# Down projection of a hybrid decoder layer: weight combinations made in place, own raw buffers for every second block, eight output spots held in PSUM

## The chip, the core and the metric

The kernel runs on one core of a Trainium2 chip. Its engines are TensorE (PE, with its weight loads as PEld), VectorE (DVE), ScalarE (ACT), GpSimd (POOL) and SyncE (SP, which here only issues transfers). Each works through a queue of its own in order. The metric is device time in microseconds of one launch, the median of several runs.

## The reference

One layer of a decoder over 1024 tokens and 16 learned ones in front, all in float32: a normalisation, one wide input projection, four token mixers (a gated recurrence, a multi-scale pooling, a stick-breaking attention, a short convolution), a gated merge with an output projection, and then the part that this change touches, with 1024 columns and 4096 hidden columns:

```python
h2 = rmsnorm(x, norm2_g)
act = jnp.square(jax.nn.relu(jnp.einsum('bld,df->blf', h2, w_up)))
return x + jnp.einsum('blf,fd->bld', act, w_down)
```

and a last normalisation of the result.

## The kernel before

Every float32 operand of a matmul is split in two (L74, L75): ACT casts it to a rounded high part, DVE subtracts that from it for the low part, and three matmuls (high with high, high with low, low with high) stand for one. DVE's operation at L75 has two SBUF inputs.

The hidden columns are 32 rows of 128. The down projection sums over them: the first 4 rows in the standard way, the other 28 by Strassen's scheme in Winograd's form, with 7 products for 8.

**Standard rows** (L948 to L963). The output is 16 spots: 8 blocks of 128 tokens by 2 halves of 512 columns, kept in SBUF in x1, which also holds the residual. `down_std` sums two rows for each spot in one PSUM bank (6 matmuls) and DVE adds the bank to x1 (L957). It is called twice, for rows 0 and 1 and for rows 2 and 3 (L1065); the second pass uses the banks "z" and "tr". There are eight banks: "mm" three, "z" two, "tr" two, "av" one. The later rows' operands were loaded early ("early", L880) and are split into the "wa" buffers at L962.

**Strassen rows** (L968 to L1104). 28 rows are 14 blocks of two, each 256 hidden columns; a group c is two blocks, so there are 7 groups. For a block, `down_w` loads two rows of w_down into w1 and w2 (L972, L973, by SP). Their halves are b11, b12 (w1) and b21, b22 (w2). The seven right-hand operands of the products are b11, b21, b22 and four combinations: b12 - b11, b22 minus that, b22 - b12, and b21 minus the second. POOL makes the four (L981, L983, L984, L988), and ACT and DVE split everything into the pair h, l of 7 x 512 columns (`put`). The pairs lie in "wb" for groups 0, 2, 4, 6 and in "wa" for the others, so those of group c + 1 can be written as soon as group c - 1 is done with them. The raw tiles w1 and w2 take the two buffers "raw"; the first two combinations go to a third tile "ta" in a buffer "hi".

A group has four units m, each for two token blocks. A unit's left-hand sums come from DRAM: `down_s` loads one tile (s_raw, one buffer) and splits it into s_hi ("wide" is its low part) and a late part ("lo" or "s_late"). Then 7 products of 6 matmuls follow; their order over two units is 1 and 5 of a unit, 7 of the unit before, 6, 2 and 3 of the unit, 4 of the unit before. DVE adds results to x1 (L1021 to L1039); product 6 accumulates in the bank that L1021 reads after product 1, so it must wait for that add.

The code's order is not the queues' order: a scheduler at build time places the instructions of each engine by priority and a model of its own. Buffers of a tag are handed round, and whoever writes one waits for the last user.

Of the kernel before, what the change touches and what calls it, by code (L numbers as in the profile page):

```python
# [10 lines left out]
F32 = mybir.dt.float32  # L11
# [6 lines left out]
P = 128  # L18
D = 1024
# [5 lines left out]
NB = T // P  # L25
# [19 lines left out]
def hybrid_trunk_kernel(ctx: ExitStack, tc: tile.TileContext, x_tok, metas, vecs, gains, w_in, w_br, w_pool,  # L45
                        w_o, w_up, w_dn, lvl_mask, out):
    nc = tc.nc

    def pool(name, bufs=1, side=None, stack=ctx):
        return stack.enter_context(tc.tile_pool(name=name, bufs=bufs, side=side, reuse_waits="tile"))  # L50

    const = pool("const")
    wst = pool("wst", 2)
# [6 lines left out]
    def nm(s):  # L60
        serial[0] += 1
        return f"{s}_{serial[0]}"

    def bank(tag):
        return psum.tile([P, 512], F32, tag=tag, name=nm(tag), bufs=PSUM_BUFS[tag])

    def new(pl, shape, dt, tag, bufs=None):
        return pl.tile(shape, dt, tag=tag, name=nm(tag), **({} if bufs is None else {"bufs": bufs}))
# [27 lines left out]
    def mm3(ps, lhs, rhs, first, last):  # L96
        lh, ll = lhs
        rh, rl = rhs
        nc.tensor.matmul(ps, lh, rh, start=first, stop=False)  # L99
        nc.tensor.matmul(ps, lh, rl, start=False, stop=False)  # L100
        nc.tensor.matmul(ps, ll, rh, start=False, stop=last)  # L101
# [96 lines left out]
    with ExitStack() as st:  # L198
# [159 lines left out]
        for i, (c0, n) in enumerate(FCH):  # L358
            last = i == len(FCH) - 1
# [25 lines left out]
        for i in range(NS + 2):  # L385
            parts, z, r = [], iter(()), i % (2 * NB)
            if i < NS:
# [9 lines left out]
                z = steps[i].scores(i)  # L397
# [50 lines left out]
    with ExitStack() as st:  # L448
# [35 lines left out]
        for hd in range(HEADS):  # L484
# [36 lines left out]
            for half in range(2):  # L521
                ps = bank("z")
# [3 lines left out]
            for li, h in enumerate(LEVELS):  # L526
# [8 lines left out]
                ps = bank("z")  # L535
# [31 lines left out]
            ps = bank("tr")  # L567
            nc.tensor.matmul(ps[:, :P], kt[:NM, NB, :], v[:NM, NB, :], start=True, stop=True)
            nc.vector.tensor_copy(S[:, NB - 1, :], ps[:, :P])
            for c1 in (NB, NB // 2):  # L570
                ps = bank("tr").rearrange("p (b c) -> p b c", c=P)
# [138 lines left out]
    with ExitStack() as st:  # L710
        p2 = pool("prep", 1, None, st)
        u = None
        for k in range(4):
# [6 lines left out]
            u = pool_diff(p2, k, v)  # L720
# [6 lines left out]
    with ExitStack() as st:  # L727
# [38 lines left out]
        for u, (n, d0) in enumerate(units):  # L766
            outs = [new(p2, [P, T], F32, "go", 3) for _ in range(2)]

            def put(r, c, ps, add):
                dst = outs[r][:, c * 512:(c + 1) * 512]  # L770
                if add is None:
                    nc.scalar.activation(dst, ps, AF.Sigmoid)
                else:
                    nc.vector.tensor_add(dst, ps, add)
                    nc.scalar.activation(dst, dst, AF.Sigmoid)
# [48 lines left out]
    with ExitStack() as st:  # L824
        x1 = new(pool("x1", 1, None, st), [P, NB, D], F32, "x1")
# [3 lines left out]
        for eh in range(2):  # L829
            es = slice(eh * 512, (eh + 1) * 512)  # L830
            wh, wl = wo0 if eh == 0 else load_wo(1, wst, "raw")
            for b in range(NB):
# [3 lines left out]
                ps = bank("mm")  # L836
# [18 lines left out]
    with ExitStack() as st:  # L855
# [41 lines left out]
        for f in range(FS):  # L897
# [4 lines left out]
            for c0, n in QCH:  # L902
                cs = slice(c0, c0 + n)
                ps = bank("mm")
# [8 lines left out]
        for f in range(FS, NF, 2):  # L913
# [17 lines left out]
            if f + 2 == NF:  # L931
                eng = nc.sync
                x1 = new(dn, [P, NB, D], F32, "x1", 1)
# [11 lines left out]
        h2stack.close()  # L945
        dw = pool("down", 4)

        def down_std(rows, tags):  # L948
            n = len(rows)
            for b in range(NB):  # L950
                bs = slice(b * P, (b + 1) * P)
                for eh in range(2):
                    es = slice(eh * 512, (eh + 1) * 512)
                    ps = bank(tags[(2 * b + eh) % len(tags)])
                    for i, (act, wd) in enumerate(rows):
                        mm3(ps, (act[0][:, bs], act[1][:, bs]), (wd[0][:, es], wd[1][:, es]), i == 0, i == n - 1)
                    nc.vector.tensor_add(x1[:, b, es], x1[:, b, es], ps)  # L957

        down_std(rows, ("z", "tr", "mm", "z", "tr", "mm", "mm"))
        act2, wd2 = (pair_of(dw, ("wa", "wa"), 4, [P, 7 * 512]) for _ in range(2))  # L960
        rows = [tuple(tuple(t[:, i * D:(i + 1) * D] for t in ab) for ab in (act2, wd2)) for i in range(2)]
        for i, t in enumerate(early):  # L962
            split(*rows[i // 2][i % 2], t)  # L963

        TI = {1: 0, 2: 1, 3: 2, 5: 3, 6: 4, 7: 5, 4: 6}
        SI = {1: 0, 5: 1, 2: 2, 6: 3, 3: 4, 7: 5, 4: 6}

        def down_w(u):  # L968
            h, l = pair_of(dw, (("wb", "wb"), ("wa", "wa"))[u // 2 % 2], 4, [P, 7 * 512])
            f = FS + 2 * u  # L970
            w1, w2 = new(wst, [P, D], F32, "raw"), new(wst, [P, D], F32, "raw")
            nc.sync.dma_start(w1, w_dn[f])  # L972
            nc.sync.dma_start(w2, w_dn[f + 1])  # L973
            b11, b12, b21, b22 = w1[:, :512], w1[:, 512:], w2[:, :512], w2[:, 512:]
            ta = new(wst, [P, D], F32, "hi")

            def put(c0, src):
                sl = (slice(None), slice(c0, c0 + src.shape[1]))
                split(h[sl], l[sl], src)

            nc.gpsimd.tensor_sub(ta[:, :512], b12, b11)  # L981
            put(0, b11)
            nc.gpsimd.tensor_sub(ta[:, 512:], b22, ta[:, :512])  # L983
            nc.gpsimd.tensor_sub(b12, b22, b12)  # L984
            put(512, w2)
            put(1536, ta)
            put(2560, b12)
            nc.gpsimd.tensor_sub(b21, b21, ta[:, 512:])  # L988
            put(3072, b21)
            return h, l  # L990

        def down_s(c, m):
# [10 lines left out]
        class Unit:  # L1003
# [7 lines left out]
            def prod(self, ps, i, fresh=False):  # L1011
                for k, (th_, tl_) in enumerate(self.tw):
                    rs, ls = slice(TI[i] * 512, (TI[i] + 1) * 512), slice(SI[i] % 5 * P, (SI[i] % 5 + 1) * P)
                    sh, sl = (t[:, k, ls] for t in self.s[SI[i] // 5])
# [47 lines left out]
                final(self.m, 1)  # L1062

        NU = (NF - FS) // 2
        down_std(rows, ("z", "tr"))  # L1065

        fg, outs = None, None

# [12 lines left out]
        prev, last = None, NU // 2 - 1  # L1081
# [83 lines left out]
```

## Time and profile before

| | us |
|---|---|
| median of three runs | 2033.37 (2032.72 to 2042.26) |
| profiled execution, its own time | 2038.52 |
| its span | 2036.8 |
| mean granted clock of TensorE in it | 0.993 |

Down projection in the profile: from 1694.89 us to the end. In the views below, L-numbers are lines of the kernel; a tile's name stands without its number; "out<-in" is what an instruction writes and reads; "[1.00 <-X]" is the idle time of the engine before it, and what ended that. In the list of stretches the columns are the length, then busy time and count for PE, PEld, DVE, ACT and POOL, the granted clock, the share of the DMA engines and GB/s (where one engine was asked for, only that one).

### The profile page before, as it was taken

The numbers are of one execution on the slowest core, as the hardware profiler recorded it, in microseconds if no ns is written. First come the engines' busy times: TensorE is split into PE (matmuls) and PEld (weight loads), VectorE is DVE, ScalarE is ACT, GpSimd is POOL, SyncE is SP. The second block draws the span as 40 slices with busy tenths as digits, with TensorE's granted clock in tenths as the row PEclk, the third lists the DMA queues.
The fourth block names the chain that finished last, engine by engine and source line by source line (L and its number), as shares of the span: only waits on it lengthen the run. The fifth ranks groups of instructions, "written<-read, shape, count | busy, mean of one in ns | idle before, by whom it ended". The sixth has DMA issues, their size and how long they took to land.

```text
span 2036.8 us, 25928 instructions
## 1 busy us (share of the span) xinstructions
PE 1947.2 (96%) x9972; PEld 1657.5 (81%) x9972; DVE 1352.2 (66%) x1797; ACT 866.2 (43%) x1481; POOL 379.1 (19%) x346
## 2 busy tenths in 40 slices
PE   7989989999999899999999999999999999899998
PEld 6778788888889898888887888887788888678876
DVE  6778887668777964333333567479555556888887
ACT  6566665433332323434433122255454553434435
POOL 3121212200010002333330000001332221432322
PEclk9999999999999999999999999999999999999999
DMA  3100000201101222332334655142445556444443
GB/s 136 42 32 22 32 32 22 69 22 42 53 22 41 72 85 77 124 120 88 124 124 174 219 181 186 48 155 82 146 135 160 162 147 232 149 138 139 160 134 131
DMA packets 109916, 216.76 MB, mean 106 GB/s; under 512 B 7888, under 2 KB 58576, under 8 KB 109792
## 3 DMA queue, kind: packets, MB, share of 16 engines
q1 hardware_dynamic: 55696, 171.54, 25.0%
q10 hardware_dynamic: 54096, 43.56, 6.5%
q8 instruction: 78, 1.28, 0.3%
q14 instruction: 46, 0.38, 0.1%
HBM read 153.73 MB, written 61.34 MB: 106 GB/s over the span
## 4 chain that ended last, share of the span: by engine, by line
PE 72%; DVE 13%; issue 6%; ACT 3%; DMA 3%; POOL 2%; SPq 0%; POOLq 0%; DVEq 0%; ACTq 0%
PE mm L672 15%; PE mm L100 10%; PE mm L101 10%; PE mm L99 10%; PE z L672 8%; PE tr L672 4%; PE mm L1016 4%; PE z L1016 2%; DVE keep L312 2%; PE z L545 1%; DMA raw<-in_w_dn_dram 1%; PE av L336 1%; PE tr L1016 1%; DVE wa L75 1%; PE tr L323 1%
## 5 line engine op out<-in xcount | busy, mean ns | idle before, releaser
L99 PE MATMUL mm<-h_hi,hi 128*128 128x384 f32 (+4 forms) x1008 | 351.9, 350 | 0.8 <-ACT a L177 0.6
L101 PE MATMUL mm<-h_hi,lo 128*128 128x384 f32 (+4 forms) x1008 | 346.7, 344 | 4.2 <-DVE lo L75 4.2
L100 PE MATMUL mm<-h_lo,hi 128*128 128x384 f32 (+4 forms) x1008 | 347.3, 345 | 0.7 <-DVE h_lo L75 0.7
L101 PEld LDWEIGHTS mm<-h_hi,lo 128*128 128x128 f32 x1008 | 191.7, 190 | 17.1 <-DVE lo L75 4.9
L100 PEld LDWEIGHTS mm<-h_lo,hi 128*128 128x128 f32 x1008 | 191.9, 190 | 12.5 <-DVE h_lo L75 1.2
L99 PEld LDWEIGHTS mm<-h_hi,hi 128*128 128x128 f32 x1008 | 191.5, 190 | 12.4 <-ACT a L177 0.9
L649 POOL TENSOR_TENSOR sf<-raw 128x512 f32<-128x512 f32 x30 | 41.7, 1390 | 784.7 <-DVE eh L615 341.4
L75 DVE TENSOR_TENSOR sl<-sf,sh 128x1024 fp32r<-128x1024 f32 x60 | 74.4, 1241 | 106.2 <-ACT sh L74 106.2
L75 DVE TENSOR_TENSOR lo<-raw,hi 128x1024 fp32r<-128x1024 f32 x79 | 98.8, 1251 | 53.2 <-ACT hi L74 43.3
L74 ACT CAST hi<-raw 128x1024 fp32r<-128x1024 f32 x79 | 83.1, 1052 | 102.9 <-PE mm L100 68.3
L99 PE MATMUL mm<-b_hi,eh 128*128 128x512 f32 x256 | 100.2, 392 | 1.9 <-DVE mixed L812 1.9
L100 PE MATMUL mm<-b_lo,eh 128*128 128x512 f32 x256 | 100.8, 394 | 0.1
L101 PE MATMUL mm<-b_hi,el 128*128 128x512 f32 x256 | 100.3, 392 | 0.5 <-DVE el L75 0.5
L672 PE MATMUL mm<-th,sh 128*128 128x512 f32 x240 | 94.1, 392 | 5.0 <-ACT cc L677 5.0
L74 ACT CAST sh<-sf 128x1024 fp32r<-128x1024 f32 x60 | 63.0, 1052 | 72.6 <-PE z L672 34.7
L672 PE MATMUL mm<-tl,sh 128*128 128x512 f32 x240 | 93.9, 391 | 0.0
L672 PE MATMUL mm<-th,sl 128*128 128x512 f32 x240 | 93.9, 391 | 0.0
L312 DVE TENSOR_TENSOR_SCAN keep<-keep 128x1039 f32<-128x1039 f32 (+3 forms) x64 | 88.9, 1393 | 6.9 <-ACT keep L305 3.3
L310 POOL TENSOR_SCALAR_AFFINE_SELECT keep<-keep 128x128 f32<-128x128 f32 x64 | 34.5, 539 | 260.2 <-ACT keep L305 225.9
L75 DVE TENSOR_TENSOR at_l<-tr,at_h 128x384 fp32r<-128x384 f32 (+2 forms) x112 | 62.6, 567 | 22.5 <-ACT at_h L74 20.1
L323 PE MATMUL tr<-ident,sig 128*128 128x128 f32 x352 | 56.6, 276 | 21.1 <-DVE sig L313 15.0
L75 DVE TENSOR_TENSOR el<-raw,eh 128x512 fp32r<-128x512 f32 x30 | 31.9, 1064 | 64.5 <-ACT eh L74 61.4
(389 smaller groups left out, 4974.7 us busy)
## 6 DMA issues: line engine op xcount, KB each, us to landing
raw<-in_w_in_dram SPq DMA_DIRECT2D x76, 512.0 KB, 3.8
s_raw<-sum_dram SPq DMA_DIRECT2D x28, 896.0 KB, 4.8
gate_dram<-go ACTq DMA_DIRECT2D x32, 512.0 KB, 2.6
go<-gate_dram SPq DMA_DIRECT2D x32, 512.0 KB, 3.4
raw<-in_w_up_dram SPq DMA_DIRECT2D x32, 512.0 KB, 3.8
raw<-in_w_dn_dram SPq DMA_DIRECT2D x31, 512.0 KB, 4.7
sum_dram<-go ACTq DMA_DIRECT2D x52, 256.0 KB, 4.5
sum_dram<-sums ACTq DMA_DIRECT2D x39, 256.0 KB, 4.6
```

Of the source, the lines that this page charges most:

```text
L74: nc.scalar.copy(hi, src)
L75: (eng or nc.vector).tensor_sub(lo, src, hi.bitcast(F32))
L99: nc.tensor.matmul(ps, lh, rh, start=first, stop=False)
L100: nc.tensor.matmul(ps, lh, rl, start=False, stop=False)
L101: nc.tensor.matmul(ps, ll, rh, start=False, stop=last)
L310: nc.gpsimd.affine_select(out=t, in_=t, compare_op=ALU.is_gt, fill=fill, base=0, pattern=[[1, P]], channel_multiplier=-1)
L312: nc.vector.tensor_tensor_scan(kp[:, 1:n], kp[:, 1:n], kp[:, 1:n], 1.0, op0=ALU.mult, op1=ALU.min)
L323: nc.tensor.transpose(ps[:, b, :], self.sg[:, (b0 + b) * P:(b0 + b + 1) * P], ident)
L336: nc.tensor.matmul(av[:, :w], pair.vv[e][:, b, :], a[:, b, :w], start=i == 0 and a is at[0], stop=i == len(order) - 1 and a is at[1])
L649: nc.gpsimd.tensor_add(s12[:, 0], a21, a22)
L672: nc.tensor.matmul(ps, lhs[i][x][:, k, :], rhs[i][y][:, k, :], start=fresh and k == 0 and n == 0, stop=k == 3 and n == 2, skip_group_check ...
L1016: nc.tensor.matmul(ps, x, y[:, rs], start=fresh and k == 0 and n == 0, stop=k == 1 and n == 2, skip_group_check=not fresh)
```

## The change

Three things. In `down_w` the four combinations are made in place: b12 - b11 overwrites b11 (L987), b22 - b12 overwrites b12 (L988), and so on (L990, L991); "ta" is gone, the splits are four in place of five (512, then three times 1024 columns), and two of the seven operands change places in the pair (the table TI). Each in-place subtraction follows the split of what it overwrites. The raw tiles of every second block (u odd) take the two buffers "hi" in place of "raw". In the standard rows the first pass finishes only spots 0 to 7; spots 8 to 15 stay in the eight banks, without an add, and the second pass adds its rows to them there first; the other eight spots of the second pass use "av", "z" and "tr". Each of the spots 8 to 15 thus has one add in place of two.

```diff
-        down_std(rows, ("z", "tr", "mm", "z", "tr", "mm", "mm"))
+        spots = [(b, slice(eh * 512, (eh + 1) * 512)) for b in range(NB) for eh in range(2)]
+
+        def down_std(rows, spot, ps, first=True, last=True):
+            b, es = spot
+            bs = slice(b * P, (b + 1) * P)
+            for i, (act, wd) in enumerate(rows):
+                mm3(ps, (act[0][:, bs], act[1][:, bs]), (wd[0][:, es], wd[1][:, es]), first and i == 0,
+                    last and i == len(rows) - 1)
+            if last:
+                nc.vector.tensor_add(x1[:, b, es], x1[:, b, es], ps)
+
+        held = []
+        for i, spot in enumerate(spots):
+            ps = bank(("z", "tr", "mm", "z", "tr", "mm", "mm", "av")[i % 8])
+            down_std(rows, spot, ps, last=i < 8)
+            if i >= 8:
+                held.append((spot, ps))
...
-        TI = {1: 0, 2: 1, 3: 2, 5: 3, 6: 4, 7: 5, 4: 6}
+        TI = {1: 0, 2: 1, 3: 2, 5: 3, 7: 4, 4: 5, 6: 6}
...
-            w1, w2 = new(wst, [P, D], F32, "raw"), new(wst, [P, D], F32, "raw")
+            w1, w2 = (new(wst, [P, D], F32, ("raw", "hi")[u % 2]) for _ in range(2))
...
-            ta = new(wst, [P, D], F32, "hi")
...
-            nc.gpsimd.tensor_sub(ta[:, :512], b12, b11)
             put(0, b11)
-            nc.gpsimd.tensor_sub(ta[:, 512:], b22, ta[:, :512])
+            put(512, w2)
+            nc.gpsimd.tensor_sub(b11, b12, b11)
             nc.gpsimd.tensor_sub(b12, b22, b12)
-            put(512, w2)
-            put(1536, ta)
-            put(2560, b12)
-            nc.gpsimd.tensor_sub(b21, b21, ta[:, 512:])
-            put(3072, b21)
+            put(1536, w1)
+            nc.gpsimd.tensor_sub(b22, b22, b11)
+            nc.gpsimd.tensor_sub(b21, b21, b22)
+            put(2560, w2)
...
-        down_std(rows, ("z", "tr"))
+        for spot, ps in held:
+            down_std(rows, spot, ps, first=False)
+        for i, spot in enumerate(spots[:8]):
+            down_std(rows, spot, bank(("av", "z", "tr")[i % 3]))
```

What the scheduler makes of it is shown at three places. The first is DVE in group 2, from the first split of a block for group 3 (wa, from raw) to the next unit's s tile (wide, lo). L1021 is the add after product 1, L1023 after 5, L1027 after 7, L1031 after 6, L1039 after 4. Before:

```order
L75 TENSOR_TENSOR wa_15137<-raw_15138,wa_15136 128x512
L1039 TENSOR_TENSOR x_2122_13999<-mm_14798,x_2122_13999 128x512
L75 TENSOR_TENSOR wa_15137<-raw_15139,wa_15136 128x1024
L1021 TENSOR_TENSOR tr_14964<-mm_14962,x_2122_13999 128x512
L1023 TENSOR_TENSOR x_2122_13999<-z_14963,x_2122_13999 128x512
L75 TENSOR_TENSOR wa_15137<-hi_15142,wa_15136 128x1024
L1027 TENSOR_TENSOR x_2122_13999<-mm_14901,x_2122_13999 128x512
L75 TENSOR_TENSOR wide_15017<-s_raw_15014,s_hi_15016 128x1280
L1031 TENSOR_TENSOR x_2122_13999<-mm_14962,x_2122_13999 128x512
L75 TENSOR_TENSOR lo_15020<-s_raw_15014,lo_15020 128x512
L75 TENSOR_TENSOR wa_15137<-raw_15138,wa_15136 128x512
```

After the change the same place reads (L1024, L1026, L1030, L1034, L1038 and L1042 are the adds after products 1, 5, 7, 6, 3 and 4):

```order
L1024 TENSOR_TENSOR tr_14930<-mm_14928,x_2122_13999 128x512
L75 TENSOR_TENSOR wa_15103<-raw_15104,wa_15102 128x512
L1026 TENSOR_TENSOR x_2122_13999<-z_14929,x_2122_13999 128x512
L75 TENSOR_TENSOR wa_15103<-raw_15105,wa_15102 128x1024
L1030 TENSOR_TENSOR x_2122_13999<-mm_14867,x_2122_13999 128x512
L75 TENSOR_TENSOR wa_15103<-raw_15104,wa_15102 128x1024
L1034 TENSOR_TENSOR x_2122_13999<-mm_14928,x_2122_13999 128x512
L75 TENSOR_TENSOR wa_15103<-raw_15105,wa_15102 128x1024
L1038 TENSOR_TENSOR x_2122_13999<-z_14929,x_2122_13999 128x512
L75 TENSOR_TENSOR wide_14983<-s_raw_14980,s_hi_14982 128x1280
L1042 TENSOR_TENSOR x_2122_13999<-mm_14867,x_2122_13999 128x512
L75 TENSOR_TENSOR lo_14986<-s_raw_14980,lo_14986 128x512
```

The block's four splits now stand together between the adds of one unit, and "wide" of the next unit stands behind the last of them; before, two of the five came after "wide".

The second place is ACT at the same point, with the casts of the high parts. Before:

```order
L74 CAST wa_15136<-raw_15138 128x512
L74 CAST wa_15136<-raw_15139 128x1024
L74 CAST wa_15136<-hi_15142 128x1024
L74 CAST wa_15136<-raw_15138 128x512
L74 CAST s_hi_15016<-s_raw_15014 128x1280
L74 CAST lo_15020<-s_raw_15014 128x512
L74 CAST wa_15136<-raw_15139 128x512
L1033 COPY x_2122_13999<-tr_14964 128x512
```

and after, where wa_15102 is the pair of the first block and wa_15120 that of the second, which is read from the buffers "hi":

```order
L74 CAST wa_15102<-raw_15104 128x512
L74 CAST wa_15102<-raw_15105 128x1024
L74 CAST wa_15120<-hi_15122 128x512
L74 CAST wa_15120<-hi_15123 128x1024
L74 CAST wa_15102<-raw_15104 128x1024
L74 CAST wa_15102<-raw_15105 128x1024
L1036 COPY x_2122_13999<-tr_14930 128x512
L74 CAST s_hi_14982<-s_raw_14980 128x1280
L74 CAST lo_14986<-s_raw_14980 128x512
```

The casts of the second block's untouched halves moved up to the first block's, and s_hi of the next unit moved behind all casts of the first block.

The third place is DVE at the passes of the standard rows. Before, from the last three adds of the first pass (mm_14128, z_14136, tr_14144) on into the second pass, with splits of rows 2 and 3 (wa) and of block 0 (wb):

```order
L957 TENSOR_TENSOR x_2122_13999<-x_2122_13999,mm_14128 128x512
L75 TENSOR_TENSOR wa_14155<-s_raw_13975,wa_14154 128x1024
L957 TENSOR_TENSOR x_2122_13999<-x_2122_13999,z_14136 128x512
L957 TENSOR_TENSOR x_2122_13999<-x_2122_13999,tr_14144 128x512
L75 TENSOR_TENSOR wa_14153<-s_late_13976,wa_14152 128x1024
L75 TENSOR_TENSOR wa_14155<-raw_13977,wa_14154 128x1024
L75 TENSOR_TENSOR wb_14293<-raw_14294,wb_14292 128x512
L957 TENSOR_TENSOR x_2122_13999<-x_2122_13999,z_14164 128x512
L957 TENSOR_TENSOR x_2122_13999<-x_2122_13999,tr_14172 128x512
L957 TENSOR_TENSOR x_2122_13999<-x_2122_13999,z_14180 128x512
```

After, at the last adds of the held spots (mm_14130, av_14137) and the first of the other eight (z_14220, av_14212), with block 0 (from raw) and block 1 (from hi):

```order
L957 TENSOR_TENSOR x_2122_13999<-x_2122_13999,mm_14130 128x512
L75 TENSOR_TENSOR wb_14277<-raw_14279,wb_14276 128x1024
L957 TENSOR_TENSOR x_2122_13999<-x_2122_13999,av_14137 128x512
L75 TENSOR_TENSOR wb_14295<-hi_14296,wb_14294 128x512
L957 TENSOR_TENSOR x_2122_13999<-x_2122_13999,z_14220 128x512
L75 TENSOR_TENSOR wb_14295<-hi_14297,wb_14294 128x1024
L957 TENSOR_TENSOR x_2122_13999<-x_2122_13999,av_14212 128x512
L957 TENSOR_TENSOR x_2122_13999<-x_2122_13999,tr_14228 128x512
L75 TENSOR_TENSOR wb_14295<-hi_14296,wb_14294 128x1024
```

Block 1's splits, which stood near the end of the second pass, now stand in its middle, and the add that frees the bank "av" stands behind the last split of block 0.

More of the change, by code (lines that the diff above doesn't have):

```diff
@@ L946, in hybrid_trunk_kernel @@
         dw = pool("down", 4)
[L948 to L957, printed above, removed]
-        down_std(rows, ("z", "tr", "mm", "z", "tr", "mm", "mm"))
+        spots = [(b, slice(eh * 512, (eh + 1) * 512)) for b in range(NB) for eh in range(2)]
[13 more added lines that the diff above has]
+                held.append((spot, ps))
         act2, wd2 = (pair_of(dw, ("wa", "wa"), 4, [P, 7 * 512]) for _ in range(2))
```

## The prediction

> **What bounds the kernel now.** First the page, for the span and the engines' shares; then the table of stretches, for how much TensorE (PE) loses in which stage; then the waits of PE alone, and the timeline around them.
>
> ```profile
> span 2036.8 us, 25928 instructions
> PE 1947.2 (96%) x9972; PEld 1657.5 (81%) x9972; DVE 1352.2 (66%) x1797; ACT 866.2 (43%) x1481; POOL 379.1 (19%) x346
> 1694.89:1738.75 43.86, 43.86 (x194) 35.97 (x193) 36.01 (x48) 12.72 (x16) 7.39 (x5) 1.00 0.69 244
> 1738.75:1784.24 45.49, 38.36 (x158) 29.92 (x156) 39.77 (x46) 20.21 (x26) 21.25 (x12) 0.96 0.41 140
> 1784.24:1985.42 201.18, 193.82 (x842) 158.35 (x840) 171.81 (x210) 83.92 (x110) 57.53 (x39) 0.99 0.41 142
> 1985.42:2036.80 51.38, 41.57 (x181) 33.44 (x179) 38.63 (x82) 25.80 (x58) 10.68 (x8) 0.96 0.36 132
> PE mm L1016 <- DVE tr L1021: 11.7, 7, 3.6
> PE mm L1016 <- ACT s_hi L74: 2.4, 1, 2.4
> ```
>
> PE sets the time. The four stretches are the two standard passes, group 0, groups 1 to 5, and group 6 with the ending. In the stretches' rows the first time is the length, then PE, PEld, DVE, ACT, POOL busy. The passes have no gap in PE. A group is 4 units of 7 products of 6 matmuls. A product takes 1.36 us, as the chain shows:
>
> ```profile
> 1872.20 2.72 PE mm L1016 x12
> 1874.92 1.36 PE z L1016 x6
> 1881.72 2.72 PE mm L1016 x12
> ```
>
> So a unit is 9.52 us and a group 38.1. Group 0 takes 45.5 and so loses 7.4; groups 1 to 5 take 201.2 against 190.4 and lose 10.8 together, 2.2 each. Most of that is the wait for the add at L1021, which VectorE (DVE) reaches late:
>
> ```profile
> 1744.19 0.50 PE L1016 MATMUL mm<-wb,s_hi 128*128 128x512 f32 x1 [2.44 <-ACT s_hi L74]
> 1744.53 0.40 PE L1016 MATMUL z<-wb,s_hi 128*128 128x512 f32 x1
> 1744.77 0.40 PE L1016 MATMUL z<-wb,wide 128*128 128x512 f32 x1
> 1746.58 0.73 PE L1016 MATMUL mm<-wb,s_hi 128*128 128x512 f32 x2 [0.72 <-DVE tr L1021]
> 1777.25 1.22 PE L1016 MATMUL mm<-wb,s_hi 128*128 128x512 f32 x2 [3.63 <-DVE tr L1021]
> 1978.23 1.15 PE L1016 MATMUL mm<-wa,s_hi 128*128 128x512 f32 x2 [2.16 <-DVE tr L1021]
> 1777.00:1778.00 1.00, 0.75 (x2) 0.50 0.00 0
> 1778.00:1779.00 1.00, 1.00 (x4) 0.50 0.00 0
> ```
>
> Of the 11.7 us in seven waits, 0.72 and 3.63 lie in group 0, which leaves 7.4 for groups 1 to 5. Behind the longest waits the granted clock is 0.50 for about 3.2 us: after 1777.25 the matmuls come every 0.43 us for 0.23, and 1.6 us are lost once more. It happened after 3.63 and after 2.16 us, and not after 2.44, where the matmuls at 1744.53 and 1744.77 are 0.24 apart. 7.4 and one such 1.6 make 9.0; the other 1.8 of the 10.8 is 0.36 a group in small pieces.
>
> **The change, part by part.** Work first. PE's matmuls are the same. DVE loses eight adds of the first pass (0.6 us each, 4.8) and one split in five per block, with the same number of columns. GpSimd (POOL) keeps four subtractions a block. None of that is on the path by itself: no pass had a gap.
>
> *Loads.* The blocks' loads waited on SP for the last use of the two raw buffers:
>
> ```profile
> SPq L972 <- DVE wb L75: 34.5, 7, 11.9
> 1887.32 1.30 POOL L981 TENSOR_TENSOR hi<-raw 128x512 f32<-128x512 f32 x1 [10.11 <-DMA raw<-in_w_dn_dram]
> 1887.81 2.16 DVE L75 TENSOR_TENSOR wide<-s_raw,s_hi 128x1280 fp32r<-128x1280 f32 x1
> 1888.69 2.42 POOL L983 TENSOR_TENSOR hi<-raw,hi 128x512 f32<-128x512 f32 x1
> ```
>
> The second block of a group now has its own two, so its load lies there early. That removes the first cause of the late L1021: the second block's subtractions and splits no longer arrive in a heap with the load. It gains at most the 18 us lost in groups 0 to 5.
>
> The last two rows also price POOL against DVE. The split at 1887.81 takes 1.48 us elsewhere (1878.81, below); here it waits 0.8 for POOL's op to end at 1888.62. POOL's next takes 2.42 for 1.30: it waits until the split is through. I take it that a DVE operation on two SBUF tensors and a POOL operation run one after the other, and that whoever waits is next.
>
> *In place.* This is the dear part. Before, the first block's three subtractions ran as soon as its load was there, long before its slots were free, with DVE half idle; one was left for the busy unit:
>
> ```profile
> 1863.12 1.29 POOL L981 TENSOR_TENSOR hi<-raw 128x512 f32<-128x512 f32 x1 [6.56 <-DMA raw<-in_w_dn_dram]
> 1865.74 1.29 POOL L984 TENSOR_TENSOR raw<-raw,raw 128x512 f32<-128x512 f32 x1
> 1872.69 1.57 ACT L74 CAST wb<-raw 128x512 fp32r<-128x512 f32 x2 [1.22 <-PE mm L1016]
> 1873.35 0.69 DVE L75 TENSOR_TENSOR wb<-raw,wb 128x512 fp32r<-128x512 f32 x1 [0.42 <-ACT wb L74]
> 1874.56 1.21 DVE L75 TENSOR_TENSOR wb<-raw,wb 128x1024 fp32r<-128x1024 f32 x1
> 1875.69 0.69 DVE L1021 TENSOR_TENSOR tr<-mm,x 128x512 f32<-128x512 f32 x1
> 1875.91 1.29 POOL L988 TENSOR_TENSOR raw<-raw,hi 128x512 f32<-128x512 f32 x1 [8.88 <-DVE wb L75]
> 1877.47 1.27 ACT L74 CAST s_hi<-s_raw 128x1280 fp32r<-128x1280 f32 x1 [1.74 <-DMA s_raw<-sum_dram]
> 1878.81 1.48 DVE L75 TENSOR_TENSOR wide<-s_raw,s_hi 128x1280 fp32r<-128x1280 f32 x1
> 1880.40 0.59 ACT L1033 COPY x<-tr 128x512 f32<-128x512 f32 x1 [0.62 <-PE tr L1016]
> ```
>
> Now the first subtraction overwrites b11, so it must wait for DVE's low part of b11, which waits for ACT's high part, which waits for the slot (1872.69). All four subtractions, 5.2 us, move behind that point. And the order of the engines puts the splits of both halves ahead of what the next unit needs: on ACT, the cast of w2 (behind POOL's fourth) stands ahead of s_hi; on DVE, the w2 split ahead of "wide". PE cannot start the next unit without s_hi.
>
> I walk it with the durations above on the clock of the group that begins at 1862.68, in the order of groups 2 to 5. Steps of DVE are 0.6 for an add or 512 columns, 1.13 for 1024, 1.40 for 1280; of ACT 1.05 for 1024, 0.5 for the copy, 1.25 for s_hi. Product 1 of the second unit ends at 1874.92; the third unit is due 6 products later, at 1883.08.
> - DVE: L1024 to 1875.6, b11 low part to 1876.2.
> - POOL 1: to 1877.6. DVE's w2 split waits for it: to 1878.7.
> - POOL 2: to 1880.0; POOL 3: to 1881.3. ACT's w1 cast to 1881.1, DVE's w1 split to 1882.4.
> - POOL 4 waits for that: to 1883.8. ACT's w2 cast to 1884.8, copy to 1885.3, s_hi to 1886.5.
>
> PE is 3.45 us late. Then 5 matmuls (1.1 us) fit in before "wide", which DVE ends at 1888.0 (w2 split to 1886.0, an add): 0.35 more, **3.8** in all. The second block repeats it one unit on: DVE has its b11 low part at 1890.6, POOL ends at 1892.0, 1894.4, 1895.7 and 1898.1, s_hi at 1901.0, and PE is free at 1896.4: **4.6**. In group 1 the order has b11 ahead of L1024, and the same walk gives 3.1 and 4.3.
>
> Sum for groups 1 to 5: 7.4 + 4 x 8.4 = 41.0 of stalls; one slow-clock stretch a group, 5 x 1.6 = 8.0; the small pieces 1.8. That is 50.8 in place of 10.8: **+40**.
>
> A rule against the row: the Trainium skill (TensorE: Matmul & The Clock Gate, "What's actually happening") halves the clock after an idle window of about 3.4 us. By it both stalls of a group would bring a slow stretch, 5 x 1.6 = 8 us more than I sum. This trace had one already after 2.16 us of idle and none after 2.44, so I stay with one a group.
>
> *Held spots and group 0.* Spots 8 to 15 keep all eight banks until the second pass ends them. Before, DVE waited for the late half of x1, and group 0 for its second block:
>
> ```profile
> 1711.77 0.69 DVE L957 TENSOR_TENSOR x<-x,tr 128x512 f32<-128x512 f32 x1 [3.92 <-DMA x<-x_dram]
> 1736.42 1.29 POOL L981 TENSOR_TENSOR hi<-raw 128x512 f32<-128x512 f32 x1 [6.55 <-DMA raw<-in_w_dn_dram]
> ```
>
> The first wait goes, but hid nothing on PE. The second, with the 2.44 that it led to, should go. But the new order puts the add of the last held spot (bank "av") behind the first block's w2 split. PE begins the second pass at 1716.65 (16 spots of 1.36 after 1694.89), ends the held spots at 1727.5, and DVE has the block's b11 low part after the third held add, at 1721.9. From there to the end of the w2 split the walk above took 9.8 us: 1731.7, and the add ends at 1732.3. PE needs the bank at 1729.1 and waits 3.3 us. The second block's chain begins after the add, at 1732.95, and ends at 1742.8; behind it stand three adds, "wide", a low part and L1024, 4.4 us, so that group 0's third product starts at 1747.2 for 1746.58. Inside group 0 the next block has its b11 at 1747.8, and s_hi of unit 2 ends at about 1757.6 where PE wants it at 1752.7 (four products on): 5.0. "Wide" comes behind parts of one block more, at about 1761.2, 2.7 later than PE wants it. So 0.6 and 7.7 come for the 3.63 and 1.6 that go: +3, and a slow stretch of 1.6 is likely. I take **+5**, between 0 (no lock, below) and +8 (more than one slow stretch).
>
> Sum: +45 on the profiled execution's 2038.52 gives 2083.5. Its time lies 5.2 above the median of the three runs, 2033.37, so the forecast against that median is **2078**.
>
> **The rivals.**
> - *The chain without the lock.* If DVE and POOL do not hold each other up, POOL runs 1876.3 to 1881.5, s_hi is 1.2 late and "wide" 0.35; at the second block 2.15. Groups 1 to 5 then lose 5 x 3.7 + 1.8 = 20.3 for 10.8, group 0 nothing: +10, **2043**. Against it stand 1887.81 and 1888.69. The Trainium skill (SBUF — State Buffer, "SBUF: two separate sides") calls this port pair an exclusive lock held for the whole instruction, by which this case cannot come; the two rows agree.
> - *The early load wins: faster.* Mechanism: the second block's load is off SP's wait, and the whole of the 18 us goes. **2015**. It decides where POOL's fourth subtraction ends before about 1880.2, so that ACT's w2 cast, copy and s_hi end by 1883.08. For it: the 34.5 us of waits of L972. Against: four subtractions of 1.29 after 1876.2 end at 1881.4 at best.
> - *Even.* Chains of 3.7 us a group, no loss in the passes, and a slow stretch less: about **2033**; it needs the first rival and gains besides.
> - *Worse.* POOL loses the port at three more places by half a split (0.6) and both stalls of a group bring the slow clock: 3.4 more in each of five groups, **2095**.
>
> **How the numbers follow.** The order in the queues is known, the durations are rows, and even the mildest walk ends on the slow side. Forecast (2065 to 2095) 0.64; no or half a lock (2043 to 2065) 0.22; faster 0.09; even 0.05. The range leaves out the faster and the even case: 2043 to 2095. Slower by over 0.5% (about what a measurement of this kernel can tell from no change) 0.86, within it 0.05, faster 0.09.
>
> **What would show it.** Right: per group two idle stretches of PE, of 3 to 5 us, ended by ACT's s_hi (or DVE's "wide"), not by the add to "tr"; POOL's first subtraction of each block released by DVE; SP's waits at the block loads no longer ahead of POOL; groups 1 to 5 about 48 us each; a wait on "av" near 1729. Wrong: groups of 38 to 40 us; s_hi landing before its unit is due; DVE splits beside POOL at 1.21.

## The result and the profile after

| | before | after |
|---|---|---|
| median of four runs each, us | 2035.32 (2032.72 to 2042.26) | 2088.89 (2086.18 to 2091.41) |
| ratio after to before | | 1.0263, 95% interval 1.0246 to 1.028 |
| profiled execution, its own time | 2038.52 | 2086.18 |
| its span | 2036.8 | 2084.4 |

The change makes the kernel slower by 2.6%. The forecast was 2078, with a range of 2043 to 2095.

The page of the changed kernel, span and busy time of the engines; then the table of the same four stretches as before (two passes, group 0, groups 1 to 5, group 6 with the ending; length, then busy time and count of PE, PEld, DVE, ACT, POOL, then granted clock, DMA share, GB/s):

```profile
span 2084.4 us, 25896 instructions
PE 1965.7 (94%) x9972; PEld 1667.8 (80%) x9972; DVE 1339.4 (64%) x1775; ACT 860.4 (41%) x1467; POOL 387.8 (19%) x346
```

```profile
1692.03:1740.56 48.53, 45.33 (x193) 37.02 (x192) 32.99 (x41) 15.35 (x18) 13.80 (x8) 0.96 0.68 240
1740.56:1786.84 46.28, 40.01 (x158) 31.41 (x156) 35.21 (x39) 16.28 (x20) 12.82 (x8) 0.89 0.41 136
1786.84:2033.30 246.46, 210.72 (x842) 167.63 (x841) 167.47 (x202) 79.94 (x100) 68.78 (x40) 0.92 0.34 111
2033.30:2084.40 51.10, 41.96 (x181) 33.25 (x179) 38.20 (x84) 25.28 (x58) 10.32 (x8) 0.97 0.38 136
```

Against before the passes take 4.67 us more (48.53 for 43.86), group 0 0.79, groups 1 to 5 45.28, and the end 0.28 less: 50.46. The passes begin 2.86 earlier (1692.03 for 1694.89), in code that the change does not touch; 50.46 less 2.86 are the 47.6 between the spans. PE does the same 9972 matmuls, but is "busy" 18.5 us longer: a matmul at half clock is a longer one, and the clock of groups 1 to 5 is 0.92 where it was 0.99.

The waits of PE in this part (in total, how often, the longest), and four of the stalls in the timeline:

```profile
PE mm L1019 <- ACT s_hi L74: 39.2, 11, 4.3
PE av L99 <- DVE x L957: 3.2, 1, 3.2
PE mm L1019 <- DVE wide L75: 2.8, 3, 1.2
```

```profile
1729.67 0.79 PE L99 MATMUL av<-wa,wa 128*128 128x512 f32 x1 [3.20 <-DVE x L957]
...
1754.38 1.22 PE L1019 MATMUL mm<-wb,s_hi 128*128 128x512 f32 x2 [4.26 <-ACT s_hi L74]
...
1757.66 0.79 PE L1019 MATMUL mm<-wb,wide 128*128 128x512 f32 x1 [1.21 <-DVE wide L75]
...
1808.49 0.73 PE L1019 MATMUL mm<-wa,s_hi 128*128 128x512 f32 x2 [2.39 <-ACT s_hi L74]
```

The wait for the add to "tr", the largest of before (11.7 us), is gone from the list. In its place stands s_hi, eleven times: once in group 0 (4.26) and twice in each of groups 1 to 5, 34.9 together, with 0.79 for "wide" 35.7. Groups 1 to 5 lose 246.46 - 190.4 = 56.1, so 20.4 more are lost beside these waits. The clock says where most of it goes. Slices of 1 us behind the first stall of group 2 (length, PE busy and count, granted clock, DMA):

```profile
1858.00:1859.00 1.00, 0.98 (x4) 1.00 0.44 41
1859.00:1860.00 1.00, 1.00 (x3) 0.54 0.80 299
1860.00:1861.00 1.00, 1.00 (x3) 0.50 0.46 184
...
1862.00:1863.00 1.00, 1.00 (x5) 0.75 0.63 211
1863.00:1864.00 1.00, 1.00 (x6) 1.00 1.03 412
```

The clock is at 0.50 for 3.41 us, and the matmuls take twice their time. Such a stretch follows nine of the ten stalls, all but that of 2.39 us at 1808.49; three of the nine are twice as long (6.83 us, from 1821.53, 1920.52 and 2019.51). PE is busy in 34.65 us of the nine, so they lose half of that, 17.3 us; the other 3.1 are small pieces.

Why s_hi is late, in the timelines of the four engines in group 2, in order of time:

```profile
1847.37 0.68 DVE L75 TENSOR_TENSOR wa<-raw,wa 128x512 fp32r<-128x512 f32 x1
...
1848.13 1.30 POOL L987 TENSOR_TENSOR raw<-raw 128x512 f32<-128x512 f32 x1 [27.93 <-DVE wa L75]
1848.57 1.94 DVE L75 TENSOR_TENSOR wa<-raw,wa 128x1024 fp32r<-128x1024 f32 x1
...
1849.51 2.15 POOL L988 TENSOR_TENSOR raw<-raw,raw 128x512 f32<-128x512 f32 x1
...
1851.74 1.29 POOL L990 TENSOR_TENSOR raw<-raw,raw 128x512 f32<-128x512 f32 x1
...
1853.11 2.13 POOL L991 TENSOR_TENSOR raw<-raw 128x512 f32<-128x512 f32 x1
...
1855.28 1.04 ACT L74 CAST wa<-raw 128x1024 fp32r<-128x1024 f32 x1 [2.54 <-POOL raw L991]
...
1856.71 1.26 ACT L74 CAST s_hi<-s_raw 128x1280 fp32r<-128x1280 f32 x1
...
1858.02 0.73 PE L1019 MATMUL mm<-wb,s_hi 128*128 128x512 f32 x2 [3.52 <-ACT s_hi L74]
```

POOL has been idle for 27.93 us when DVE has the low part of b11. Four subtractions take 7.1 us, two of them 2.1 for 1.3, because a DVE split is at work. ACT is idle 2.54 us until the fourth is done, casts w2, copies "tr" (at 1856.23, not shown), and only then casts s_hi, for whose input it does not wait. PE has been idle since 1854.50.

### The profile page after: what moved, and what is told of

Read it like the earlier page. It is cut to its first block, busy times and chain, and to the rows that moved or that the text cites. A ratio compares the mean times of both kernels' runs of the same rounds, so it can differ in the third digit from the quotient of the medians.

```text
span 2084.4 us, 25896 instructions
## 1 busy us (share of the span) xinstructions
PE 1965.7 (94%) x9972; PEld 1667.8 (80%) x9972; DVE 1339.4 (64%) x1775; ACT 860.4 (41%) x1467; POOL 387.8 (19%) x346
```

## The experiments

Each was compared with the kernel before on the same chip.

**1 and 2: one part alone.** Held spots with the blocks of before; and the blocks of the change with the standard rows of before (the diff above, split in two).

> Only the held spots of the change; the blocks' combinations and buffers are those of before. My theory: the late add to the bank 'av' came from the in-place chain that stands ahead of it, so the held spots alone cost nothing: passes of 43.9 to 45 us with no wait on 'av' above 1 us, groups 1 to 5 as before (201 us), 2030 to 2042 us in all. Rival (holding the eight banks costs by itself, because PE gets a bank only after the add): a wait on 'av' of about 3 us stays, with a slow-clock stretch, and the time is 4 to 9 above before, 2039 to 2045 us.

> Only the block part of the change (in place, own buffers for odd blocks); the standard rows are those of before. My theory: groups 1 to 5 keep their ten stalls (ACT s_hi) and take 246 us for 201, so the time is 2078 to 2086 us (the 4 to 8 us of the passes and group 0 gone or changed). Rival (the two parts add up otherwise, the held spots shift the groups and so cause part of the stalls): groups 1 to 5 below 230 us, time below 2068 us.

Held spots alone: 2030.75 us, ratio 0.9979 (0.997 to 0.9988). In place and own buffers alone: 2085.01, ratio 1.0245 (1.0229 to 1.026). The stretches of the held spots alone (passes, group 0, groups 1 to 5), and the waits of the other kernel:

```profile
1691.16:1735.75 44.59, 44.14 (x193) 35.88 (x192) 33.85 (x42) 15.30 (x18) 10.89 (x8) 1.00 0.69 245
1735.75:1776.93 41.18, 36.28 (x158) 29.00 (x156) 37.48 (x44) 17.64 (x23) 14.89 (x10) 1.00 0.43 149
1776.93:1977.47 200.54, 192.25 (x841) 157.22 (x840) 171.67 (x210) 84.00 (x110) 58.96 (x40) 1.00 0.42 142
```

```profile
PE mm L1014 <- ACT s_hi L74: 36.8, 11, 3.8
```

The loss comes with the blocks: 49.8 of the 53.6 us. Holding the spots by itself costs waits of at most 0.2 us on "av" and saves 4.4 us. Only together with the in-place blocks does it cost something (2088.89 for 2085.01, with intervals that overlap): then the chain stands ahead of the last held spot's add on DVE, and PE waits 3.20 us for "av".

**3: in place, without own buffers.**

```diff
-            w1, w2 = (new(wst, [P, D], F32, ("raw", "hi")[u % 2]) for _ in range(2))
+            w1, w2 = (new(wst, [P, D], F32, "raw") for _ in range(2))
```

> The change without the own buffers: all blocks use the two buffers 'raw', combinations in place. My theory: the chain behind the in-place subtraction is the whole loss and the early load only softens it; without it the second block's load begins when the first block's last split is through and lands some 6.5 us later, so the second stall of a group grows by 2 to 4 us, 5 x 2 to 4 above the change: 2097 to 2112 us. Rival 1 (the early load is what collides: with both blocks' data there, the casts of the second block crowd ACT and DVE): the stalls shrink and the time is below 2080 us. Rival 2 (the load never matters): 2086 to 2092 us.

2082.32 us, ratio 1.0232 (1.0215 to 1.025): 6.6 faster than the change, where I had expected 8 to 23 slower (the two intervals still touch, 1.0246 being the lower end for the change). My theory of the load fell; neither rival's range has this time either. The stretches of group 0 and of groups 1 to 5; then, in the timeline of group 2, DVE's add after product 1, its low part of the second block's b11, and POOL's first subtraction of that block:

```profile
1738.62:1780.19 41.57, 37.92 (x158) 28.66 (x156) 33.75 (x39) 17.65 (x21) 13.00 (x9) 1.00 0.50 164
1780.19:2027.91 247.72, 213.20 (x842) 169.46 (x840) 166.50 (x202) 80.44 (x100) 68.83 (x40) 0.91 0.35 113
```

```profile
1854.85 0.70 DVE L1024 TENSOR_TENSOR tr<-mm,x 128x512 f32<-128x512 f32 x1 [1.15 <-PE mm L1019]
1855.46 0.68 DVE L75 TENSOR_TENSOR wa<-raw,wa 128x512 fp32r<-128x512 f32 x1
...
1856.22 1.29 POOL L987 TENSOR_TENSOR raw<-raw 128x512 f32<-128x512 f32 x1 [8.06 <-DVE wa L75]
```

Groups 1 to 5 take the same (247.72 for 246.46). POOL's first subtraction waits there for DVE, and DVE for PE's product 1, not for a load: the first stall of a group delays everything, and I take it that the load has time under it. So the early load bought nothing in the groups. In group 0 it cost 4.7 us (46.28 for 41.57): without it s_hi of unit 2 stands on ACT ahead of the block's w2 cast and begins 9.7 us after the group (1748.32 less 1738.62), in the change 12.5 (1753.07 less 1740.56).

**4: another order.** The edit gives nothing but the place of some splits in the queues of ACT and DVE, and the scheduler then puts some adds, and the second block's first splits, elsewhere on DVE as well; `issue_after` queues an instruction behind another of its engine and adds no wait.

```diff
-            def put(c0, src):
+            def put(c0, src, late=False):
                 sl = (slice(None), slice(c0, c0 + src.shape[1]))
-                split(h[sl], l[sl], src)
+                with ExitStack() as behind:
+                    if late and u > 1:
+                        for ins in s_ops[(u // 2 - 1) * 4 + 2 + u % 2]:
+                            behind.enter_context(tc.issue_after(ins))
+                    split(h[sl], l[sl], src)
...
-            put(1536, w1)
+            put(1536, w1, True)
...
-            put(2560, w2)
+            put(2560, w2, True)
```

(`u` is the block, two to a group; `s_ops` holds the two instructions that make s_hi and "wide" of each unit.)

> The change with another order in two queues and nothing else: from group 1's blocks on, the casts and low parts of the two combination halves of a block stand on ACT and DVE behind s_hi and 'wide' of the next unit, not ahead of them. POOL's chain and its wait for the low part of b11 stay as they are. My theory (the loss is the queue order: s_hi stands behind a cast that waits for POOL's fourth subtraction): the stalls on s_hi of groups 1 to 5 go, with their slow clock, 45 to 56 us less than the change: 2030 to 2046 us, groups of 38 to 41 us. Rival 1 (the chain itself is too long: the products need its results): new stalls of PE on the pair 'wa' or 'wb' at a group's start, 2055 to 2080 us. Rival 2 (POOL and DVE collide on their port and DVE is late wherever the splits stand): stalls on 'wide' or on the add to 'tr' of 2 us and more in each unit, above 2060 us.

2036.67 us, ratio 1.0008 (0.9998 to 1.0017): 52.2 us less than the change. Its stretch of groups 1 to 5 and its longest waits:

```profile
1780.33:1982.29 201.96, 194.40 (x842) 156.25 (x841) 173.81 (x203) 81.64 (x100) 75.63 (x40) 1.00 0.41 136
```

```profile
PE mm L1026 <- DVE wide L1007: 4.8, 3, 2.6
PE mm L1026 <- DVE tr L1031: 3.7, 5, 1.2
```

The wait for s_hi is gone, the clock is 1.00, and groups 1 to 5 take 201.96 us for 201.18 before. The in-place chain is still there, and POOL still waits for DVE at the head of it; it costs no more than what the groups lost before, once s_hi does not stand behind it. That is the loss of the groups, shown by its removal. (The wait of 3.2 us on "av" in the passes stays.)

**5: the order kept, the chain gone.** The change without its four subtractions; it leaves the combinations out and splits the raw halves in their place, so its output is not the layer's.

> The change without its four subtractions a block on POOL: the combinations are left uncomputed and the raw halves are split in their place. The order of DVE's queue is the same, and on ACT s_hi still stands behind all casts of the block. My theory (the loss needs both: the order, and the chain low part of b11, four subtractions, casts): without the chain ACT's casts end by about 1880 on the clock of the group at 1862.68, s_hi by 1881.5, before its unit is due at 1883.08, so no stalls on s_hi and 2028 to 2042 us; DVE's splits of 1024 take 1.21 to 1.34 us where they took 1.94. Rival (s_hi is late because of the casts themselves or of DVE's splits, not of POOL): stalls of 2 us and more per unit stay, above 2060 us.

2017.93 us (two runs). The stretch of groups 1 to 5, and the split that took 1.94 us in the change:

```profile
1772.96:1964.59 191.63, 191.50 (x842) 157.00 (x840) 157.17 (x201) 79.20 (x100) 0.00 (x0) 1.00 0.44 143
1824.72 1.22 DVE L75 TENSOR_TENSOR wa<-raw,wa 128x1024 fp32r<-128x1024 f32 x1
```

Groups of 38.3 us, PE without a gap, though s_hi still stands behind all casts of the block. So the loss needs both, the order and the chain (of which POOL's work beside DVE is a part that no run takes away alone); and a DVE split of two SBUF inputs takes 1.22 with POOL still, 1.94 beside it.

**6: one subtraction less behind the wait.** Other formulas for the same operands.

```diff
+            nc.gpsimd.tensor_sub(b12, b22, b12)
             put(0, b11)
             put(512, w2)
-            nc.gpsimd.tensor_sub(b11, b12, b11)
-            nc.gpsimd.tensor_sub(b12, b22, b12)
+            nc.gpsimd.tensor_add(b11, b11, b12)
             put(1536, w1)
             nc.gpsimd.tensor_sub(b22, b22, b11)
-            nc.gpsimd.tensor_sub(b21, b21, b22)
+            nc.gpsimd.tensor_sub(b21, b21, b11)
```

> The change with other formulas for the same seven operands: b22 - b12 overwrites b12 first, which waits for no split, so three operations in place of four stand behind the low part of b11 (b11 + b12, then two that subtract it). The order of DVE's queue is the same, on ACT only the copy of 'tr' changes places. My theory (the stall is as long as the chain behind b11's low part): by the rows of the change for its third group, the third of the three ends about 2.2 us earlier than the fourth of four (1855.2), less what a collision with DVE's split costs again, so s_hi is 1.3 to 2.2 us earlier and the stalls are 1.3 to 2.2 us in place of 3.5; at most half of them still bring a slow clock: 2052 to 2070 us. Rival 1 (ACT's casts, not POOL, set s_hi): the stalls stay at 3 us and more, 2080 to 2090 us. Rival 2 (the early operation collides with DVE elsewhere and the gain is given back at the adds): 2070 to 2080 us.

2069.44 us, ratio 1.0185 (1.0167 to 1.0203): 19.5 less than the change, at the upper end of what my theory gave; two of the four runs lie above it, where rival 2 begins. Two stalls, and POOL's operations ahead of a first one:

```profile
1912.30 1.22 PE L1019 MATMUL mm<-wa,s_hi 128*128 128x512 f32 x2 [2.88 <-ACT s_hi L74]
...
1944.64 0.72 PE L1019 MATMUL mm<-wb,s_hi 128*128 128x512 f32 x2 [1.98 <-ACT s_hi L74]
```

```profile
1844.28 1.29 POOL L988 TENSOR_TENSOR raw<-raw 128x512 f32<-128x512 f32 x1 [19.41 <-DVE wa L75]
1846.80 1.29 POOL L990 TENSOR_TENSOR raw<-raw,raw 128x512 f32<-128x512 f32 x1 [1.23 <-DVE wa L75]
1848.05 2.27 POOL L991 TENSOR_TENSOR raw<-raw,raw 128x512 f32<-128x512 f32 x1
```

The first stall of groups 2 to 5 falls from 3.5 to between 1.98 and 2.29 us: one operation less stands in the chain, but also a new wait of 1.23 for DVE's split of w2, so that it takes 6.0 us (1844.28 to 1850.32) for 7.1. The second stall is gone in groups 2 and 4, and 2.8 to 3.3 in the others, where I had expected at most 2.2. Seven of the eight stalls were followed by a slow clock, where I had expected at most half; only one of 1.35 us was not.

**7 and 8: PE kept busy in the stalls.** 14 matmuls more, whose result nobody reads, ahead of the two units of a group that stall. In the second kernel PE, ACT and DVE are besides held to the order of the change by a list.

```diff
...
             def one(self):
+                if self.m >= 2 and self.c < last:
+                    ps = bank("av")
+                    for i in range(14):
+                        h = self.tw[0][0]
+                        tc.keep_in_program_order(nc.tensor.matmul(ps, h[:, :P], h[:, :512], start=i == 0, stop=i == 13))
                 self.prod(self.al, 1, True)
...
```

> The change, and ahead of product 1 of the third and fourth unit of groups 0 to 5 (where PE waits for s_hi) 14 matmuls more of 128x512 into the bank 'av', which nobody reads: 3.2 us at 0.227 us each, 12 x 3.2 = 38 us of work in all. The other queues' order moves by single places. Theory A (the stalls are 35.7 us of groups 1 to 5, and another 18.6 us are the slow clock that follows idle PE): the added work lies inside the stalls of 3.4 to 4.1 us, leaves 0.3 to 1 us idle, the granted clock stays at 1.0 there, and the time falls by 12 to 22 us, to 2067 to 2077 us. Theory B (the clock falls for another reason than idle time, or the slow stretches only hide other waits): the clock is at 0.5 in the same places and the time is 2085 to 2092 us. Theory C (the stalls are not waits of a fixed length, PE's lateness pushes s_hi too): the added work adds to the stalls, 2105 us and more.

> The same 14 matmuls ahead of the third and fourth unit of groups 0 to 5 as in the run before, but with the queues of PE, ACT and DVE pinned to the order that they have in the change, so that nothing else differs. Theory A (idle time of PE brings the slow clock, and that is the term that the forecast sized too small): 3.2 us of added work lie inside stalls of 3.4 to 4.1 us, s_hi comes when it came before, no slow stretch is left in groups 1 to 5, groups of about 45.5 us (38.1 and two stalls of 3.6) for 49.3, and the time falls by 15 to 22 us against the change, to 2067 to 2074 us. Theory B (the slow clock has another cause): clock at 0.5 in the same places, 2086 to 2092 us. Theory C (a full clock makes units shorter, but DVE and ACT are then late again by as much): no slow stretches, but longer stalls or new ones, 2080 to 2090 us.

The first gave 2090.71 and decides nothing. The time is one that theory B names, but its sign, the clock at 0.5 in the same places, is not there (0.97 over groups 1 to 5, against 0.92 in the change); the order on DVE is another, and so are the waits (14.1 us for the add to "tr", six times). The second: 2077.81 us, ratio 1.0217 (1.0201 to 1.0232), that is 38 us of useless work added and 11.1 us less time. Its groups 1 to 5, and the added work with what is left of a first and a second stall:

```profile
1791.27:2024.11 232.84, 227.09 (x982) 182.16 (x980) 166.77 (x200) 80.31 (x100) 68.99 (x40) 1.00 0.36 118
```

```profile
1856.22 3.33 PE L1028 MATMUL av<-wb 128*128 128x512 f32 x14
1859.93 0.73 PE L1019 MATMUL mm<-wb,s_hi 128*128 128x512 f32 x2 [0.38 <-ACT s_hi L74]
...
1874.13 0.73 PE L1019 MATMUL mm<-wb,s_hi 128*128 128x512 f32 x2 [0.69 <-ACT s_hi L74]
```

The clock is 1.00 and the five groups take 232.84 for 246.46. The mechanism of theory A is shown: with PE kept busy no slow stretch is left, and the groups are 13.6 us shorter. Its time is missed (2067 to 2074): I had expected groups of 45.5 and they take 46.6. In group 2 some 0.35 of the 1.1 is "wide", late behind the fifth matmul of the first restart; the rest is not settled.

**9 and 10: a version that is faster.** The order spread further: a block's untouched halves in the second unit, the combinations of the first and second block behind "wide" of the third and fourth.

```diff
...
+            for k, (w1, w2) in enumerate(raws):
+                put(k, 0, w1[:, :512])
+                put(k, 512, w2)
+            for k, (w1, w2) in enumerate(raws):
+                b11, b12, b21, b22 = w1[:, :512], w1[:, 512:], w2[:, :512], w2[:, 512:]
+                behind = s_ops[(c - 1) * 4 + 2 + k] if c else (adds[LATE[k]],)
+                nc.gpsimd.tensor_sub(b11, b12, b11)
+                nc.gpsimd.tensor_sub(b12, b22, b12)
+                put(k, 1536, w1, behind)
+                nc.gpsimd.tensor_sub(b22, b22, b11)
+                nc.gpsimd.tensor_sub(b21, b21, b22)
+                put(k, 2560, w2, behind)
...
```

(`raws` holds the raw tiles of the two blocks, and `put` queues a split behind the instructions it is given; `adds` are the adds of the standard rows, and `LATE` picks the last held spot's and the fourth after it.)

> The change with a third order: both blocks' untouched halves are split first (second unit), the combination halves of the first block behind s_hi and 'wide' of the third unit, those of the second block behind those of the fourth; in the passes, the combination halves of block 0 stand on DVE behind the last held spot's add, those of block 1 behind the fourth add after it. My theory (with the order right, own buffers and held spots are worth what the diff gives them: early load, fewer adds, no heap of DVE work in one unit): no wait of 1 us on s_hi, 'wide' or 'av', groups of 38.1 to 39 us, 2014 to 2026 us, below before and below the held spots alone. Rival 1 (DVE is the bound of a unit, work moved only moves the wait): waits on the add to 'tr' or on 'wide' as before, 2027 to 2040 us. Rival 2 (the second block's data is late for the next group): waits of PE on 'wa' or 'wb', above 2040 us.

2036.23 us, ratio 1.0003 (0.9993 to 1.0012). A miss: my range ended at 2026. In the passes the second block's first splits now stood on DVE ahead of the add that frees "av", and one of them waited 2.2 us there for ACT's cast. The groups 1 to 5 take 39.8 us each, where I had expected 39 at most.

```profile
PE av L99 <- DVE x L958: 4.1, 1, 4.1
```

In the last kernel the two blocks of group 0 are combined apart from their data, in a third tile and with shared raw buffers, as before:

```diff
...
+            nc.gpsimd.tensor_sub(ta[:, :512], b12, b11)
+            nc.gpsimd.tensor_sub(ta[:, 512:], b22, b12)
+            nc.gpsimd.tensor_sub(b12, b22, ta[:, :512])
...
+            nc.gpsimd.tensor_sub(b21, b21, b12)
...
```

> The spread order of the run before from group 1 on; the two blocks of group 0 are combined apart from their data (a third tile, shared raw buffers), so that the passes and group 0 have no in-place chain. My theory (what was left over was the in-place chain in the passes, where DVE has 0.7 us to spare per spot): no wait on 'av' above 0.5 us, group 0 as with the held spots alone, groups 1 to 5 of 39.3 us each or less, 2022 to 2029 us, below before and below the held spots alone (2030.75). Rival (DVE is as full as it can be, the waits move on to the adds): 2030 to 2038 us, no difference to before.

2025.11 us, ratio 0.996 (0.9948 to 0.9973), 0.4% faster than before, and faster than the change. Its group 0 and groups 1 to 5:

```profile
1735.18:1774.49 39.31, 36.30 (x157) 29.09 (x156) 35.48 (x42) 16.72 (x21) 17.46 (x9) 1.00 0.50 166
1774.49:1970.65 196.16, 193.87 (x842) 156.06 (x840) 164.11 (x200) 81.69 (x100) 81.34 (x40) 1.00 0.42 139
```

Groups of 39.2 us, 5.0 us less for the five than before, and 6.2 in group 0. Its interval overlaps that of the held spots alone (0.997 to 0.9988) by a little.

## Why the prediction was right, and what it mis-sized

- **The place and the mechanism** were right: two stalls a group, ended by s_hi, behind ACT's w2 cast and POOL's fourth subtraction. Experiments 4 and 5 show both halves of it, the order and the chain, each by taking it away.
- **Groups 1 to 5:** forecast +40, measured +45.28. The stalls were forecast at 41.0 and measured at 35.7. The first was walked as 3.45 and "wide" 0.35; the rows show 3.52 or 3.53 in groups 2 to 5, with "wide" hardly late. The second was walked as 4.6 and is 3.4 to 4.1; why it is shorter is not settled. The sum comes so near in part by luck: the stalls were taken 5.3 too long, the slow clock 9.3 and the small pieces 1.3 too short.
- **The mis-sized term is the slow clock:** one stretch of 1.6 a group, 8.0 in all, in the sum; 17.3 by the rows, in nine stretches for five, three of them twice as long. Experiment 8 removes them and gets back 13.6 us of the 56.1; what the restarts cost stays. The step that failed is the one that weighed the page against the row: "This trace had one already after 2.16 us of idle and none after 2.44, so I stay with one a group." The stalls walked were of 3.1 to 4.6 us, and the one row of such a length, 3.63, had brought a slow stretch. By the rule of the Trainium skill (TensorE: Matmul & The Clock Gate, "What's actually happening") both stalls of a group would bring one. They did, nine times in ten. The text had priced this at 8 us more, in its case "worse" (2095), of which only this half came true. What tells 2.16 from 2.44 is in the last section.
- **Passes and group 0:** forecast +5, measured 4.67 + 0.79 = 5.46. The wait on "av" was walked as 3.3 and is 3.20; s_hi of unit 2 as 5.0 and is 4.26; "wide" 2.7, and is 1.21. That the total agrees is luck in part: these two waits in group 0 were taken 2.2 us too long, and the slow clock, taken as one stretch of 1.6, is one of 3.41 us in the passes and one of 10.24 in group 0 (from 1753.27), which lose 5.5 together.
- **A misread row:** "Group 0 takes 45.5 and so loses 7.4" counts 28 products. Group 0's stretch has 26 (158 matmuls in the row, where groups 1 to 5 have 842), because products 7 and 4 of its last unit run in the next; it lost 10.1. The forecast does not use the 7.4, but "at most 18 us" and the 2015 do.
- **"The chain without the lock"** (2043) fell: POOL's operations of 1.29 take 2.15 and 2.13 and DVE's split 1.94, where it takes 1.22 with POOL still. By these rows POOL's four lose 1.7 us to it, half of a stall; no run takes this part away alone. "Even" needed this rival and fell with it.
- **"The early load wins"** (2015) fell, and so did the gain of "at most 18 us" that its wait was given: experiment 3 shows no gain of the own buffers in the groups. Yet the 2018 of experiment 5, a kernel without the combinations, is about the time that it named, and shows what the waits of before are worth where no chain is left.
- **The signs named** are in the profile: two stalls a group, no first subtraction of POOL's that waits for a load, a wait on "av" at 1729.67, groups of 49.3 us for "about 48". POOL's first subtraction is released by DVE at the first block of each group; at the second the trace names no releaser (six times of seven), but in group 2 it starts at 1863.17, right after DVE's low part (1863.04).
- **Against the median:** the forecast took 5.2 us off because the profiled execution of before lay above its median. That of after lies 2.7 below its own. Of the 10.9 us by which 2088.89 is above the forecast, 5.5 are the terms above; the rest is the scatter of executions, the 5.2 and the 2.7 less the 2.86 by which the passes began earlier, and 0.4 of rounding in the 2078.

## What to carry to other kernels

An operand that is overwritten in place makes its writer wait for every earlier reader, and what this costs is decided by the in-order queues: with s_hi behind the chain's last cast it was 52 us more here than with s_hi ahead of it. A wait taken off one queue (the load) is worth only what the next cause leaves of it. Sum a stall of TensorE together with the slow clock that may follow: of the 56.1 us lost in groups 1 to 5, 17.3 were clock.

## What the runs showed of the hardware

The granted clock changes only at the borders of a grid. In each of the twelve traces of this case the changes lie whole multiples of 3.41 us apart, and a slow stretch is one, two or three such windows at 0.50. Whether a stall brings one depends on how much of it falls into one window. In experiment 6 the stall of 1.98 us that ends at 1989.83 lies whole in one window and was followed by a slow one; with the held spots alone a border cuts the stall of 3.44 us that ends at 1771.36 in two, and the clock stayed. It was so in the kernel before: the 2.16 us lay in one window, the 2.44 us were cut at 1742.81. The windows of the one and of the other (length, PE busy and count, granted clock, DMA):

```profile
1983.57:1986.98 3.41, 3.41 (x16) 1.00 0.18 73
1986.98:1990.40 3.42, 1.44 (x7) 1.00 0.00 0
1990.40:1993.81 3.41, 3.34 (x9) 0.50 0.00 0
```

```profile
1766.29:1769.70 3.41, 1.62 (x8) 1.00 0.85 268
1769.70:1773.12 3.42, 1.76 (x8) 1.00 0.00 1
1773.12:1776.53 3.41, 3.41 (x17) 1.00 0.91 296
```

From 1690 to 2010 us of the twelve traces there is no exception: after a window at full clock in which PE was idle for 1.98 us or more (53 windows) the next was at 0.50, after one with 1.87 or less it stayed at 1.00. A window at 0.50 was followed by another when PE was idle for 0.59 us or more in it (17 windows), and by full clock at 0.58 or less (52). So here a stall of under 1.87 us alone brings no slow clock and one of 4 us always does (an estimate: twice 1.98); in between it is chance, by where the border falls. By the same figures a stall of 3.5 us escapes only when a border cuts it almost in the middle, in about one position of eight (an estimate too). The bounds are those of this stage; near 700 us, in other code, the clock fell after less idle time (1.42 us at the least).

The page of the Trainium skill named above (TensorE: Matmul & The Clock Gate, "What's actually happening") describes a free-running window of about 3.4 us, and the traces agree with it. But by its idle time of about 3.4 us the 1.98 should have brought no slow clock; here the measurement decides.
